# Other blocks with seven products for eight, exponentials three steps later, and norm rows in 8 KB tiles

## The chip, the cores and the metric

The kernel runs on one core of a Trainium2 chip. The metric is the device time of one execution in microseconds, the median of several runs. TensorE multiplies matrices, VectorE and ScalarE do elementwise work, GpSimd does a little of it, and SP (SyncE) issues nearly all transfers from HBM, in the order of the program.

## What is computed

One layer of a streaming encoder over 256 tokens of width 2048, all in float32. With h = layer norm of x, the core of the reference is:

```python
proj = h @ w_in + b_in                       # 2048 x 14400
q, k, v, og, fg, u, z, ga, gb = split(proj)
log_a = log_sigmoid(fg @ w_f2 + b_f2) / 16   # decays, cumulated over chunks of 64 tokens
o = gla_chunk_causal(q, k, v, log_a)         # exp of the decays, states, scores
y_a = rms_norm(o, gla_norm_g) * silu(og)
y_b = gelu(u) * (w_s @ layer_norm(gelu(z), gmlp_ln) + b_s)
m = sigmoid(ga) * y_a + sigmoid(gb) * y_b
h = layer_norm(ALPHA * h + m @ w_o, ln1)
ffn = (silu(gate) * up) @ w_down             # gate, up = split(h @ w_gu), width 5632
ple = sigmoid(h @ w_pg + b_pg) * (p @ w_pu)
out = layer_norm(ALPHA * h + ffn + ple, ln2)
```

## The kernel before

Every weight comes once from HBM in float32, in pieces of 128 x 1024 (two k-tiles of 128 rows by 512 columns). A "split" turns a piece into a high part on ScalarE (a copy to fp32r, L217) and a low part on VectorE (piece minus high part, L218). A product is then three matmuls: high by high, low by high, high by low. A matmul here takes 128 tokens by 512 columns, so a step of `token_block` (one piece, two token halves of 128) has 2 x 2 x 3 = 12 matmuls.

`pair_block` takes two column blocks of 512 at once. For `s` of its k-pairs it forms the 2 x 2 product (token halves by column blocks, over an even and an odd k-tile) with seven products in place of eight, by sums and differences of weights (on VectorE, L448, L480, L483, in place in the raw tile) and of activations (made once per stage by `sums`, on VectorE and one ScalarE copy, L378). The remaining k-pairs go the plain way (`std`). The steps of a seven-product group are short: five splits, a to e, whose steps have 3 to 9 matmuls; two PSUM banks are seeded from a third by ScalarE copies (L414), and two are copied out (L419). This front part of a block is called its head below. The last plain step of a pair block is held back (`pending`) and put behind the first steps of the next block.

The whole program is a list of steps (`steps`), walked by `pump`. Step by step it emits splits ahead, as long as `limit["hl"]` split tiles are in use, and loads ahead, as long as `limit["raw"]` raw tiles are. `before(c, fn)` hangs work before step c, `soon(n, fn)` n steps behind the steps added so far, and `later(n, fn)` n steps behind the one being walked. Evacuations of PSUM are `jobs`, one or two behind each step. SP and GpSimd run in the order in which the program emits; the other engines are ordered by the framework's scheduler from the priorities of that order.

All large tiles (raw and split weights, activations, sums) are slots of one ring of 21 tiles of 8 KB per partition (`slot`, NSLOT). Work tiles of 2 KB come from a ring of nine (`t2`, NT2). A bias or norm row, broadcast to 128 partitions for two column blocks (1024 columns), is a 4 KB tile from a ring of three (`rowvec`, tag "bc", L109 to L115), loaded by SP at L114; a load into this ring waits on SP until the tile's last reader is done, and SP's later loads wait behind it.

The order of the stages is: start (norm of x, transposes), v, fg (two steps, after which the decays are computed piecemeal: `decay_logits`, `decay_log`, `decay_scan`, `decay_ends`, `decay_exp` at set steps), q, k, og with the attention between its steps, z, u, gb, ga, wo, pu, pg, and then four parts of gate/up blocks (gu) followed by the part's down blocks (dn). `residual` scales the normed stream by its gain and adds its bias on GpSimd (L634, L635), four operations per column block, for ln0 during v and q, and for ln1 during pg. Before the change seven products are used with s = 2 in the last two blocks of og, in u, gb, the first two blocks of ga, and the last two of pg, and with s = 3 in gu; v, z, wo and down go the plain way.

Of the kernel before, what the change touches and what calls it, by code (L numbers as in the profile page):

```python
# [42 lines left out]
def block_kernel(ctx: ExitStack, tc: tile.TileContext, x, p, ln0_g, ln0_b, w_in, b_in, w_f2, b_f2,  # L43
# [251 lines left out]
    def token_block(src, nk, xT, evac, name, held=None, halves=False):  # L295

        flush()
        st = {"w": {}}  # L300
# [12 lines left out]

        def size(i):
            return min(KC, nk - i * KC)

        def mk(i):
            def consume(hi, lo):
                if i == 0:
                    st["ps"] = [acc(f"{name}_{t}") for t in range(NT)]  # L320
                st["w"][i] = (hi, lo)
                keep = h0_ <= i < h1_
                final = i == nchunk - 1
                one(i, size(i), 0)
                if final:
                    if keep:
                        evac(0, st["ps"][0])
                    else:
                        jobs.append(lambda: evac(0, st["ps"][0]))
                if not keep:  # L330
                    one(i, size(i), 1)
                elif i == h1_ - 1 and halves:
                    for j in range(2):
                        ps = st["ps"][1] if j == 0 else acc(f"{name}_1b")
                        for ii in range(h0_, h1_):
                            one(ii, size(ii), 1, j * 256, (j + 1) * 256, ps)
                        evac(1, ps, j)
# [199 lines left out]
    def soon(n, fn):  # L537
        before(len(steps) + n, fn)
# [122 lines left out]
    def ws_job():  # L661
# [9 lines left out]
        nc.scalar.activation(wsT[0], wt, AF.Copy)  # L671
        nc.vector.tensor_tensor(out=wsT[1], in0=wt, in1=wsT[0].bitcast(F32), op=ALU.subtract)


    def v_evac(b):
        def evac(t, ps, add=None):
            if "v" not in G:
                G["v"] = [[slot(f"v{i}_{tt}", F32R) for tt in range(NT)] for i in range(2)]
            a = t2(f"av{b}_{t}")
            nc.vector.tensor_tensor(out=a, in0=ps, in1=rowvec("bv", b_in, C_V, b), op=ALU.add)  # L680
            vh, vl = (x[t][:, b * CB:(b + 1) * CB] for x in G["v"])
            nc.scalar.activation(vh, a, AF.Copy)
# [136 lines left out]
    def decay_ends():  # L819
# [5 lines left out]
        for m in range(NCH - 1):  # L825
            nc.vector.tensor_copy(es[:, :, m, m + 1], be[:, :, m + 1])
            for n in range(m + 2, NCH):
                nc.vector.tensor_tensor(out=es[:, :, m, n], in0=es[:, :, m, n - 1], in1=be[:, :, n],
                                        op=ALU.add)
        nc.scalar.activation(es, es, AF.Exp, scale=1.0 / TAU)  # L830
        G["es"], G["be"] = es, be

    def decay_exp(i):
        (mn, lg), be = G["dec"], G["be"]
        n = 4 * NCH
        sl = slice(i * 1024, (i + 1) * 1024)
        bev = be.rearrange("p t n -> p (t n)")[:, i * n:(i + 1) * n].unsqueeze(2).broadcast_to([P, n, CH])
        m = mn[:, sl].rearrange("p (g c) -> p g c", c=CH)
        nc.vector.tensor_tensor(out=m, in0=bev, in1=m, op=ALU.subtract)
        nc.scalar.activation(lg[:, sl], mn[:, sl], AF.Exp, scale=1.0 / TAU)  # L840

    def decay_steps():
        later(2, decay_logits)
# [149 lines left out]
            nc.vector.tensor_tensor(out=y, in0=y, in1=a, op=ALU.mult)  # L993
        return evac

    def s0():
        return G["s0"]
# [5 lines left out]
    before(len(steps) - 3, lambda: G.update(s0=sums(h0T, S_IN, "s0")))  # L1003
    before(len(steps), lambda: limit.update(raw=4, hl=5))
    pairs(w_in, C_OG, h0T, og_evac, "og", S_IN, s0, (2,), [("b_og", b_in, C_OG)])

    def z_evac(b):
        def evac(t, ps, add=None):
            if b == 0 and t == 0:
# [4 lines left out]
            nc.vector.bn_stats(out=st[:, 0, :], in_=a)  # L1014
            mv, r = ln_finish(st, 1, f"zln{b}_{t}")
            nc.vector.scalar_tensor_tensor(out=a, in0=a, scalar=mv[:, 0:1],
                                           in1=rowvec("gmg", gm_g, 0, b), op0=ALU.subtract,
                                           op1=ALU.mult)
            nc.vector.scalar_tensor_tensor(out=a, in0=a, scalar=r[:, 0:1],
                                           in1=rowvec("gmb", gm_b, 0, b), op0=ALU.mult, op1=ALU.add)  # L1020

            w = []

# [14 lines left out]
            later(11, mix)  # L1038
        return evac

    pairs(w_in, C_Z, h0T, z_evac, "z", S_Z, s0, (0, 2), [("b_z", b_in, C_Z), ("gmg", gm_g, 0), ("gmb", gm_b, 0)])

    def yb_evac(key, c0, b, fn):
        def evac(t, ps, add=None):
# [3 lines left out]
            nc.vector.tensor_tensor(out=y, in0=y, in1=a, op=ALU.mult)  # L1048
        return evac

    pairs(w_in, C_U, h0T, lambda b: yb_evac("u", C_U, b, AF.Gelu), "u", S_IN, s0, (0, 2), [("b_u", b_in, C_U)])
    pairs(w_in, C_GB, h0T, lambda b: yb_evac("gb", C_GB, b, AF.Sigmoid), "gb", S_IN, s0, (0, 2), [("b_gb", b_in, C_GB)])

    def ga_evac(b):
# [31 lines left out]
                ln_norm(h0[t], h0[t], st1[t], f"ln1_{t}")  # L1086
        return evac

    for b in range(4):
        token_block(wcols(w_o, b * CB), KT, lambda: G["mT"], wo_evac(b), f"wo{b}",  # L1090
                    held=(4, 8) if b == 3 else None)

# [117 lines left out]
        nc.sync.dma_start(out[t * P:(t + 1) * P, 3 * CB:], y[:, 3 * CB:])  # L1210

    def down_evac(b, last):
        def evac(t, ps, half=None):
            c0, c1 = (0, CB) if half is None else (half * 256, (half + 1) * 256)
            r = r1[t][:, b * CB:(b + 1) * CB]
            nc.vector.tensor_tensor(out=r[:, c0:c1], in0=r[:, c0:c1], in1=ps[:, c0:c1], op=ALU.add)
            if last:
                for c in range(c0, c1, 256):
                    nc.vector.bn_stats(out=st2[t][:, (b * CB + c) // 256, :], in_=r[:, c:c + 256])
# [29 lines left out]
    pump(8)
    with tc.manual_schedule(engines={ET.Activation}):  # L1250
# [33 lines left out]
```

## Time and profile before

| | us |
|---|---|
| median of 3 runs | 1605.48 (1602.62 to 1607.34) |
| the profiled execution, own time | 1605.97 |
| its span in the trace | 1603.8 |
| TensorE busy | 1565.2 (98%) |
| VectorE busy | 1159.4 (72%) |
| ScalarE busy | 817.5 (51%) |
| GpSimd busy | 92.5 (6%) |

Busy times are sums over the span, and the stages differ in which engine is short. TensorE's ends are modelled, so the number of matmuls in a stretch says more than its busy share. The granted clock of TensorE was 0.99 of full over the span. All transfers together moved 315 MB, 197 GB/s in the mean.

### The profile page before, as it was taken

The numbers are of one execution on the slowest core, as the hardware profiler recorded it, in microseconds if no ns is written. First come the engines' busy times: TensorE is split into PE (matmuls) and PEld (weight loads), VectorE is DVE, ScalarE is ACT, GpSimd is POOL, SyncE is SP. The second block draws the span as 40 slices with busy tenths as digits, with TensorE's granted clock in tenths as the row PEclk, the third lists the DMA queues.
The fourth block names the chain that finished last, engine by engine and source line by source line (L and its number), as shares of the span: only waits on it lengthen the run. The fifth ranks groups of instructions, "written<-read, shape, count | busy, mean of one in ns | idle before, by whom it ended". The sixth has DMA issues, their size and how long they took to land.

```text
span 1603.8 us, 19476 instructions
## 1 busy us (share of the span) xinstructions
PE 1565.2 (98%) x7393; PEld 1306.4 (81%) x7393; DVE 1159.4 (72%) x1359; ACT 817.5 (51%) x1026; POOL 92.5 (6%) x69
## 2 busy tenths in 40 slices
PE   8998999999999999999979999999999999999996
PEld 7888988888788888888858788888888888888885
DVE  7668448856888887673897787578775888658875
ACT  5445446644655655542635656445553565535650
POOL 1022000001100000000360000000000000000002
PEclk9999999999999999999989999999999999999998
DMA  8554545765565656674635565545575455755561
GB/s 303 199 190 149 198 153 195 278 230 165 189 205 209 205 194 231 207 246 145 209 119 209 210 210 213 183 156 183 210 262 179 149 187 195 262 184 180 190 233 53
DMA packets 160568, 315.45 MB, mean 197 GB/s; under 512 B 9789, under 2 KB 12762, under 8 KB 160218
## 3 DMA queue, kind: packets, MB, share of 16 engines
q1 hardware_dynamic: 160410, 314.18, 57.1%
q8 instruction: 58, 0.95, 0.2%
q14 instruction: 36, 0.29, 0.1%
q10 hardware_dynamic: 64, 0.02, 0.0%
HBM read 312.06 MB, written 2.10 MB: 196 GB/s over the span
## 4 chain that ended last, share of the span: by engine, by line
issue 48%; PE 22%; POOL 2%; DVE 2%; DMA 1%; ACT 0%; SPq 0%; POOLq 0%
PE gb_C L408 5%; PE u_C L408 5%; PE ga_C L408 3%; PE wo L293 2%; PE wo L291 2%; PE wo L292 2%; PE ga L292 1%; PE ga L291 1%; PE ga L293 1%; POOL xs L635 1%; POOL xs L634 1%; DVE xs L1206 0%; DMA ln1g<-in_ln_g_dram 0%; DVE xs L1204 0%; PE mtp L574 0%
## 5 line engine op out<-in xcount | busy, mean ns | idle before, releaser
L218 DVE TENSOR_TENSOR w_s<-raw,w_s 128x1024 fp32r<-128x1024 f32 x464 | 564.4, 1231 | 283.6 <-ACT w_s L217 280.6
L217 ACT ACTIVATE w_s<-raw 128x1024 fp32r<-128x1024 f32 x464 | 482.8, 1056 | 396.2 <-PE dn L293 94.4
L408 PE MATMUL gu_C<-w_s,h1Th 128*128 128x512 f32 x880 | 283.7, 390 | 0.2
L408 PEld LDWEIGHTS gu_C<-w_s,h1Th 128*128 128x128 f32 x880 | 165.0, 188 | 35.2 <-DVE w_s L218 1.4
L408 PE MATMUL gu_C<-w_s,h1Tl 128*128 128x512 f32 x440 | 171.6, 390 | 0.0
L292 PE MATMUL dn<-w_s,act 128*128 128x512 f32 (+1 forms) x352 | 136.5, 388 | 0.0
L293 PE MATMUL dn<-w_s,act 128*128 128x512 f32 (+1 forms) x352 | 136.2, 387 | 0.0
L291 PE MATMUL dn<-w_s,act 128*128 128x512 f32 (+1 forms) x352 | 136.2, 387 | 0.0
L408 PEld LDWEIGHTS gu_C<-w_s,h1Tl 128*128 128x128 f32 x440 | 82.6, 188 | 17.1
L408 PE MATMUL z_C<-w_s,h0Th 128*128 128x512 f32 x256 | 79.6, 389 | 0.0
L291 PEld LDWEIGHTS dn<-w_s,act 128*128 128x128 f32 x352 | 66.1, 188 | 13.5
L293 PEld LDWEIGHTS dn<-w_s,act 128*128 128x128 f32 x352 | 66.1, 188 | 13.4
L292 PEld LDWEIGHTS dn<-w_s,act 128*128 128x128 f32 x352 | 66.1, 188 | 13.2
L557 POOL TENSOR_TENSOR ln_r<-ln_v,mhalf 128x1 f32<-128x1 f32 x6 | 4.2, 694 | 1115.9 <-DVE ln_v L552 1115.9
L408 PE MATMUL u_C<-w_s,h0Th 128*128 128x512 f32 x192 | 62.4, 396 | 2.4 <-DVE w_s L218 2.4
L408 PE MATMUL gb_C<-w_s,h0Th 128*128 128x512 f32 x192 | 61.1, 389 | 0.0
L448 DVE TENSOR_TENSOR raw<-raw 128x1024 f32<-128x1024 f32 x47 | 58.5, 1266 | 0.5
L408 PEld LDWEIGHTS z_C<-w_s,h0Th 128*128 128x128 f32 x256 | 48.1, 188 | 9.9
L292 PE MATMUL v<-w_s,h0Tl 128*128 128x512 f32 x128 | 50.0, 390 | 0.9 <-POOL h0Tl L581 0.9
L291 PE MATMUL v<-w_s,h0Th 128*128 128x512 f32 x128 | 50.4, 394 | 0.0
L291 PE MATMUL wo<-w_s,mTh 128*128 128x512 f32 x128 | 50.0, 391 | 0.0
L293 PE MATMUL v<-w_s,h0Th 128*128 128x512 f32 x128 | 49.9, 391 | 0.0
(485 smaller groups left out, 3218.1 us busy)
## 6 DMA issues: line engine op xcount, KB each, us to landing
raw<-in_w_in_dram SPq DMA_DIRECT2D x226, 512.0 KB, 4.7
raw<-in_w_gu_dram SPq DMA_DIRECT2D x176, 512.0 KB, 4.5
raw<-in_w_down_dram SPq DMA_DIRECT2D x88, 512.0 KB, 5.0
raw<-in_w_o_dram SPq DMA_DIRECT2D x32, 512.0 KB, 4.8
raw<-in_w_pg_dram SPq DMA_DIRECT2D x32, 512.0 KB, 5.0
xs<-in_x_dram SPq DMA_DIRECT2D x4, 512.0 KB, 5.0
raw<-in_w_pu_dram SPq DMA_DIRECT2D x4, 512.0 KB, 4.4
out_dram<-xs SPq DMA_DIRECT2D x8, 256.0 KB, 2.0
```

Of the source, the lines that this page charges most:

```text
L217: nc.scalar.activation(hi, src, AF.Copy)
L218: nc.vector.tensor_tensor(out=lo, in0=src, in1=hi.bitcast(F32), op=ALU.subtract)
L291: nc.tensor.matmul(ps, lhsT=xh, rhs=wh, start=start, stop=False, **kw)
L292: nc.tensor.matmul(ps, lhsT=xl, rhs=wh, start=False, stop=False, **kw)
L293: nc.tensor.matmul(ps, lhsT=xh, rhs=wl, start=False, stop=stop, **kw)
L408: nc.tensor.matmul(ps, lhsT=a, rhs=b, start=first and j == 0 and n == 0, stop=n == 2, skip_group_check=True)
L448: nc.vector.tensor_tensor(out=r[:, 0:4:2, :], in0=r[:, 0:4:3, :], in1=r[:, 2, :].unsqueeze(1).broadcast_to([P, 2, CB]), op=ALU.subtract)
L557: nc.gpsimd.tensor_tensor(out=r[:, :n], in0=v[:, :n], in1=mhalf[:, :n], op=ALU.pow)
L634: nc.gpsimd.tensor_tensor(out=y, in0=y, in1=gt, op=ALU.mult)
L635: nc.gpsimd.tensor_tensor(out=y, in0=y, in1=bt, op=ALU.add)
```

## The change

- Seven products for eight, `s` of them: v's last two blocks (2), wo's first two (2), and in down one per pair of blocks for all parts but the last two blocks of the last part. Not any more in pg (all four blocks are token blocks) and the first two blocks of u.
- `sums` is called for v, wo and each part of down as well; for gu it stays in pg, before the first step of pg's last block.
- The limits of raw and split tiles are set to 4 and 5 around the new blocks, to 5 and 5 at the head of each part of gu.
- The three exponentials of the decays are issued three steps later.
- The rows of ln0, ln1 and of z's norm are loaded by `row2`: gain and bias for two column blocks lie in one slot of the big ring. The ring of 4 KB rows has two tiles in place of three, the ring of work tiles seven in place of nine, the big ring 22 in place of 21.

```diff
-S_IN, S_Z, S_GA, S_PG, S_FF = 2, 0, 2, 2, 3
+S_V, S_IN, S_U0, S_GA, S_WO, S_PG, S_FF, S_DN = 2, 2, 0, 2, 2, 0, 3, 1
-NSLOT = 21
-NT2 = 9
+NSLOT = 22
+NT2 = 7
@@ rowvec
-            rows_t[k] = tmp.tile([P, 2 * CB], F32, tag="bc", name=f"{key}{b // 2}", bufs=3)
+            rows_t[k] = tmp.tile([P, 2 * CB], F32, tag="bc", name=f"{key}{b // 2}", bufs=2)
+    def row2(name, srcs, i, b):
+        k = name, b // 2
+        if k not in rows_t:
+            rows_t[k] = slot(f"{name}r{b // 2}")
+            for j, src in enumerate(srcs):
+                o = b // 2 * 1024
+                nc.sync.dma_start(rows_t[k][:, j * 1024:(j + 1) * 1024],
+                                  src[o:o + 1024].partition_broadcast(P))
+        return rows_t[k][:, i * 1024 + b % 2 * CB:i * 1024 + (b % 2 + 1) * CB]
@@ residual
-        gt, bt = rowvec(f"{name}g", g, 0, c), rowvec(f"{name}b", b, 0, c)
+        gt, bt = (row2(name, (g, b), i, c) for i in range(2))
@@ v
-    for b in range(4):
+    for b in range(2):
         token_block(wcols(w_in, C_V + b * CB), KT, h0T, v_evac(b), f"v{b}", held=(0, 2) if b == 0 else None)
+        before(len(steps) - 4, lambda: G.update(s0=sums(h0T, S_V, "sv")))
+        before(len(steps), lambda: limit.update(raw=4, hl=5))
+        pairs(w_in, C_V, h0T, v_evac, "v", S_V, s0, (2,), [("bv", b_in, C_V)])
+        flush()
+        before(len(steps), lambda: limit.update(raw=3, hl=4))
@@ decay_ends, decay_exp
-        nc.scalar.activation(es, es, AF.Exp, scale=1.0 / TAU)
+        later(3, lambda: nc.scalar.activation(es, es, AF.Exp, scale=1.0 / TAU))
-        nc.scalar.activation(lg[:, sl], mn[:, sl], AF.Exp, scale=1.0 / TAU)
+        later(3, lambda: nc.scalar.activation(lg[:, sl], mn[:, sl], AF.Exp, scale=1.0 / TAU))
@@ z, u
-    pairs(w_in, C_Z, h0T, z_evac, "z", S_Z, s0, (0, 2), [("b_z", b_in, C_Z), ("gmg", gm_g, 0), ("gmb", gm_b, 0)])
+    soon(8, lambda: gm_row(0, 0))
+    pairs(w_in, C_Z, h0T, z_evac, "z", 0, s0, (0,), [("b_z", b_in, C_Z)])
+    soon(8, lambda: gm_row(0, 2))
+    pairs(w_in, C_Z, h0T, z_evac, "z", 0, s0, (2,), [("b_z", b_in, C_Z)])
-    pairs(w_in, C_U, h0T, ..., "u", S_IN, s0, (0, 2), [("b_u", b_in, C_U)])
+    pairs(w_in, C_U, h0T, ..., "u", S_U0, s0, (0,), [("b_u", b_in, C_U)])
+    pairs(w_in, C_U, h0T, ..., "u", S_IN, s0, (2,), [("b_u", b_in, C_U)])
@@ wo
-    for b in range(4):
+    before(len(steps) - 5, lambda: G.update(sm=sums(G["mT"], S_WO, "sm")))
+    before(len(steps), lambda: limit.update(raw=4, hl=5))
+    pairs(w_o, 0, lambda: G["mT"], wo_evac, "wo", S_WO, lambda: G["sm"], (0,))
+    flush()
+    before(len(steps), lambda: limit.update(raw=3, hl=4))
+    for b in range(2, 4):
@@ pg
-    for b in range(2):
+    for b in range(4):
+        if b == 2:
+            soon(3, lambda: rowvec("b_pg", b_pg, 0, 2))
         token_block(wcols(w_pg, b * CB), KT, h1T_get, pg_evac(b), f"pg{b}", ...)
-    before(len(steps) - 4, lambda: G.update(s1=sums(h1T["x"], S_FF, "s1")))
-    before(len(steps), lambda: limit.update(raw=S_FF + 2, hl=5))
-    pairs(w_pg, 0, h1T_get, pg_evac, "pg", S_PG, s1, (2,), [("b_pg", b_pg, 0)])
+    before(len(steps) - 8, lambda: G.update(s1=sums(h1T["x"], S_FF, "s1")))
@@ each part of gu and down
+        before(len(steps), lambda: limit.update(raw=S_FF + 2, hl=5))
...
+        if S_DN:
+            before(len(steps) - 6, lambda part=part: G.update(sd=sums(G["act", part], S_DN, f"sd{part}")))
+            before(len(steps), lambda: limit.update(raw=4, hl=5))
+        for b in (0, 2):
+            if S_DN and (part < 3 or b == 0):
+                pair_block(src[b:b + 2], npair * 4, act,
+                           (down_evac(b, part == 3), down_evac(b + 1, part == 3)),
+                           f"dn{part}_{b}", S_DN, lambda: G["sd"])
+        if part < 3 and S_DN:
+            continue
-        for b in range(4):
+        for b in range(2 if S_DN else 0, 4):
```

The evacuations of v and down take the copied-out bank as a further addend (`add`), one more VectorE operation in two of four evacuations of a pair.

## Rows read from the trace of the kernel before

**Rows 1.** The page's totals: busy us, share of the span, instructions, by engine.
```profile
PE 1565.2 (98%) x7393; PEld 1306.4 (81%) x7393; DVE 1159.4 (72%) x1359; ACT 817.5 (51%) x1026; POOL 92.5 (6%) x69
```
**Rows 2.** TensorE's waits: line, releaser, us in total, times, longest.
```profile
PE pg_C L408 <- ACT pg_C L414: 4.4, 1, 4.4
PE q L292 <- DVE w_s L218: 4.0, 2, 2.6
PE pg_C L408 <- DVE pg_b_s L218: 2.5, 1, 2.5
PE u_C L408 <- DVE w_s L218: 2.4, 1, 2.4
PE pg L293 <- DVE w_s L218: 2.3, 1, 2.3
...
PE gu_C L408 <- ACT gu_c_s L217: 0.3, 1, 0.3
```
**Rows 3.** Stretches: busy (count) of PE, PEld, DVE, ACT, POOL; PEclk, DMA, GB/s.
```profile
140.00:160.00 20.00, 15.99 (x119) 15.58 (x118) 18.75 (x42) 7.34 (x10) 4.66 (x5) 0.91 0.25 80
410.00:430.00 20.00, 17.10 (x67) 13.38 (x66) 18.51 (x31) 11.74 (x18) 4.29 (x4) 0.91 0.47 155
813.00:843.00 30.00, 19.55 (x64) 14.33 (x63) 28.38 (x25) 12.67 (x16) 14.82 (x8) 0.77 0.45 150
880.00:895.00 15.00, 14.60 (x62) 11.14 (x61) 14.66 (x21) 8.92 (x13) 0.00 (x0) 1.00 0.42 144
502.00:582.00 80.00, 80.00 (x354) 66.26 (x353) 63.70 (x71) 46.73 (x57) 0.00 (x0) 1.00 0.67 230
...
180.00:203.00 23.00, 23.00 (x194) 23.00 (x193) 10.86 (x13) 8.24 (x8) 0.00 (x0) 1.00 0.53 179
```
**Rows 4.** SP's queue in pg, in order of time: start, us, entry.
```profile
786.59 7.73 SPq L226 DMA_DIRECT2D raw<-in_w_pg_dram  x6
808.77 0.34 SPq L114 DMA_DIRECT2D ln1g<-in_ln_g_dram  x1
...
814.57 30.95 SPq L226 DMA_DIRECT2D raw<-in_w_pg_dram  x10
```
**Rows 5.** ScalarE in pg, in order of time, idle time in brackets.
```profile
814.51 1.49 ACT L378 ACTIVATE s_sh<-s_f 128x1536 fp32r<-128x1536 f32 x1 [14.32 <-DVE s_f L372]
```
**Rows 6.** VectorE in pg, in order of time.
```profile
795.99 1.21 DVE L218 TENSOR_TENSOR w_s<-raw,w_s 128x1024 fp32r<-128x1024 f32 x1
...
800.73 3.47 DVE L1149 TENSOR_TENSOR a_pg<-a_pg,pu 128x512 f32<-128x512 f32 x2
...
807.51 2.84 DVE L360 TENSOR_TENSOR s_full<-h1Th,h1Tl 128x1536 f32<-128x1536 f32 x1
...
816.04 2.29 DVE L379 TENSOR_TENSOR s_sl<-s_f,s_sh 128x1536 fp32r<-128x1536 f32 x1 [1.62 <-ACT s_sh L378]
818.25 2.28 DVE L218 TENSOR_TENSOR w_s<-raw,w_s 128x1024 fp32r<-128x1024 f32 x1
```
**Rows 7.** GpSimd in pg: the first and the last of 16 operations.
```profile
787.04 11.31 POOL L634 TENSOR_TENSOR xs<-xs,ln1g 128x512 f32<-128x512 f32 x1 [21.62 <-DMA ln1g<-in_ln_g_dram]
...
827.34 2.13 POOL L635 TENSOR_TENSOR xs<-xs,ln1b 128x512 f32<-128x512 f32 x1
```
**Rows 8.** VectorE's groups, 1000 to 1100 us: busy us, mean ns, idle before.
```profile
L218 DVE TENSOR_TENSOR w_s<-raw,w_s 128x1024 fp32r<-128x1024 f32 x34 | 41.4, 1223 | 28.9 <-ACT w_s L217 28.9
...
L448 DVE TENSOR_TENSOR raw<-raw 128x1024 f32<-128x1024 f32 x3 | 3.6, 1220 | 0.0
...
L480 DVE TENSOR_TENSOR raw<-raw 128x512 f32<-128x512 f32 x3 | 2.0, 682 | 0.0
```
**Rows 9.** VectorE's scans, 132 to 147 us and 147 to 150 us.
```profile
L816 DVE TENSOR_TENSOR_SCAN dmn<-dmn,dlg 128x64 f32<-128x64 f32 x24 | 12.1, 573 | 1.1 <-ACT dlg L810 1.1
...
L816 DVE TENSOR_TENSOR_SCAN dmn<-dmn,dlg 128x64 f32<-128x64 f32 x8 | 1.6, 260 | 0.0
```
**Rows 10.** The last exponential on ScalarE and its reader on VectorE.
```profile
175.75 1.05 ACT L840 ACTIVATE dlg<-dmn 128x1024 f32<-128x1024 f32 x1
...
191.94 1.66 DVE L888 SCALAR_TENSOR_TENSOR kT<-k,rows_cols,dlg 128x256 f32<-128x256 f32 x4 [5.61 <-PE k L293]
```

More of the change, by code (lines that the diff above doesn't have):

```diff
@@ L336, in consume @@
                             one(ii, size(ii), 1, j * 256, (j + 1) * 256, ps)
-                        evac(1, ps, j)
+                        evac(1, ps, half=j)
                 elif i == h1_ - 1:
@@ L672, in ws_job, with s0 @@
         nc.vector.tensor_tensor(out=wsT[1], in0=wt, in1=wsT[0].bitcast(F32), op=ALU.subtract)
+    def s0():
+        return G["s0"]
     def v_evac(b):
@@ L679, in evac @@
             a = t2(f"av{b}_{t}")
+            if add is not None:
+                nc.vector.tensor_tensor(out=a, in0=ps, in1=add, op=ALU.add)
+                ps = a
             nc.vector.tensor_tensor(out=a, in0=ps, in1=rowvec("bv", b_in, C_V, b), op=ALU.add)
@@ L684, in v_evac @@
         return evac
-    for b in range(4):
+    for b in range(2):
         token_block(wcols(w_in, C_V + b * CB), KT, h0T, v_evac(b), f"v{b}", held=(0, 2) if b == 0 else None)
+    if S_V:
+        before(len(steps) - 4, lambda: G.update(s0=sums(h0T, S_V, "sv")))
[3 more added lines that the diff above has]
+        before(len(steps), lambda: limit.update(raw=3, hl=4))
+    else:
+        for b in range(2, 4):
+            token_block(wcols(w_in, C_V + b * CB), KT, h0T, v_evac(b), f"v{b}")
     for c in range(4):
@@ L994, in og_evac @@
         return evac
-    def s0():
-        return G["s0"]
     soon(4, lambda: rowvec("b_og", b_in, C_OG, 0))
@@ L1005, in block_kernel, with gm_row @@
     pairs(w_in, C_OG, h0T, og_evac, "og", S_IN, s0, (2,), [("b_og", b_in, C_OG)])
+    def gm_row(i, b):
+        return row2("gm", (gm_g, gm_b), i, b)
     def z_evac(b):
@@ L1016, in evac @@
             nc.vector.scalar_tensor_tensor(out=a, in0=a, scalar=mv[:, 0:1],
-                                           in1=rowvec("gmg", gm_g, 0, b), op0=ALU.subtract,
+                                           in1=gm_row(0, b), op0=ALU.subtract,
                                            op1=ALU.mult)
             nc.vector.scalar_tensor_tensor(out=a, in0=a, scalar=r[:, 0:1],
-                                           in1=rowvec("gmb", gm_b, 0, b), op0=ALU.mult, op1=ALU.add)
+                                           in1=gm_row(1, b), op0=ALU.mult, op1=ALU.add)
             w = []
@@ L1049, in yb_evac @@
         return evac
-    pairs(w_in, C_U, h0T, lambda b: yb_evac("u", C_U, b, AF.Gelu), "u", S_IN, s0, (0, 2), [("b_u", b_in, C_U)])
+    pairs(w_in, C_U, h0T, lambda b: yb_evac("u", C_U, b, AF.Gelu), "u", S_U0, s0, (0,), [("b_u", b_in, C_U)])
+    pairs(w_in, C_U, h0T, lambda b: yb_evac("u", C_U, b, AF.Gelu), "u", S_IN, s0, (2,),
+          [("b_u", b_in, C_U)])
     pairs(w_in, C_GB, h0T, lambda b: yb_evac("gb", C_GB, b, AF.Sigmoid), "gb", S_IN, s0, (0, 2), [("b_gb", b_in, C_GB)])
@@ L1087, in wo_evac @@
         return evac
-    for b in range(4):
+    before(len(steps) - 5, lambda: G.update(sm=sums(G["mT"], S_WO, "sm")))
[3 more added lines that the diff above has]
+    before(len(steps), lambda: limit.update(raw=3, hl=4))
+    for b in range(2, 4):
         token_block(wcols(w_o, b * CB), KT, lambda: G["mT"], wo_evac(b), f"wo{b}",
@@ L1212, in down_evac, with evac @@
     def down_evac(b, last):
-        def evac(t, ps, half=None):
+        def evac(t, ps, add=None, half=None):
             c0, c1 = (0, CB) if half is None else (half * 256, (half + 1) * 256)
@@ L1216, in evac @@
             nc.vector.tensor_tensor(out=r[:, c0:c1], in0=r[:, c0:c1], in1=ps[:, c0:c1], op=ALU.add)
+            if add is not None:
+                nc.vector.tensor_tensor(out=r, in0=r, in1=add, op=ALU.add)
             if last:
@@ L1240, in block_kernel @@
         before(len(steps) + (npair - 1) * 2, lambda: run_jobs(100))
-        for b in range(4):
-            src = w_down[k_first * P:(k_first + npair * 4) * P, b * CB:(b + 1) * CB].rearrange(
-                "(kt p) c -> p kt c", p=P)
+        src = [w_down[k_first * P:(k_first + npair * 4) * P, b * CB:(b + 1) * CB].rearrange(
+            "(kt p) c -> p kt c", p=P) for b in range(4)]
+        act = lambda part=part: G["act", part]
+        if S_DN:
[9 more added lines that the diff above has]
+        for b in range(2 if S_DN else 0, 4):
             last = part == 3 and b == 3
@@ L1246, in block_kernel @@
                 before(len(steps) - 6, load_gb2)
-            token_block(src, npair * 4, lambda part=part: G["act", part], down_evac(b, part == 3),
+            token_block(src[b], npair * 4, act, down_evac(b, part == 3),
                         f"dn{part}_{b}", held=(0, 4) if last else None, halves=last)
```

## The prediction

> **What bounds the kernel now.** I read the page's totals first: TensorE is busy 98% of the span [rows 1], so only two things can shorten it, fewer matmuls or less time in which TensorE stands still or runs slowly. The second view is TensorE's own list of waits [rows 2]. It is short, and the reader is to see that nearly all of it lies at three places: q (4.0 us), the first u block (2.4), and pg (4.4, 2.5 and 2.3). The third view, busy time by stretch, prices these places in full, half clock included, because it counts matmuls [rows 3]. In the undisturbed gb stretch 354 matmuls of 512 columns take 80 us, 0.226 us each; in the late q and k stretch 194, all of 256 columns, take 23 us, 0.119 us each. What a stretch takes beyond its count is lost:
>
> - q, 140 to 160 us: 20.0 - 119 x 0.119 = 5.8 us.
> - z to u, 410 to 430: 20.0 - 67 x 0.226 = 4.9 us.
> - pg, 813 to 843: 30.0 - 64 x 0.226 = 15.5 us, at a granted clock of 0.77 on average (part of it at 1.2 GHz in place of 2.4).
> - gu0, 880 to 895: 15.0 - 62 x 0.226 = 1.0 us.
>
> Together 27 us, against some 1,560 us of matmuls. The fourth view is what the other engines did there. In pg, SP issued six weight loads by 794.3 us, and its next entry, a row tile of ln1, left at 808.8, after a wait of 14.4 us for one of three row buffers; the weight loads behind it left from 814.6 on [rows 4]. ScalarE stood for 14.3 us before its copy in `sums` (L378) [rows 5], because VectorE's six operations of `sums` ran from 807.5 to 818.3, each beside the residual on GpSimd [rows 6, 7]. So three things meet in pg: `sums`, the residual's rows in SP's queue, and the head of a seven-product block, which wants many splits for few matmuls.
>
> **The change part by part.**
>
> *Matmuls.* A seven-product group (one pair of k-tiles, two token halves, two column blocks) has 7 x 3 = 21 matmuls in place of 24, so it saves 3. Added groups: v 2, wo 2, down seven blocks of 1: 11, so -33 matmuls. Removed: pg 2, u0 2: +12. Net -21 x 0.226 = **-4.7 us**. No other matmul changes, and all these lie on the path, TensorE being the bound.
>
> *pg.* It becomes four plain blocks; `sums` moves from 12 to 24 steps behind pg's start, 12 x 12 x 0.226 = 32.5 us later: from 807.5 to about 840, when the residual, which ended at 829.5, is over. It issues no DMA; the ln1 rows come, two loads at a time as before, in two 8 KB slots of the big ring, which at that place has room (xs 2, pu 2, h1T 4, raw 3, split 4 and rows 2 make 17 of 22). SP's 14.4 us wait and ScalarE's 14.3 us wait go. What is late next is VectorE beside GpSimd: the 16 residual operations remain (787.0 to 829.5 us) [rows 7]. Beside them a split takes 2.28 us where one just before took 1.21, and a 512-column product 1.73 where 0.68 is the free price [rows 6, 8]. A plain block asks in 8 x 12 x 0.226 = 21.7 us for 8 x 2.28 + 4 x 1.73 + 2 x 0.69 = 26.5 us of VectorE. Over the 31 us of overlap VectorE falls 7 us behind; its lead is three steps, 8.1 us. Bounds: nothing is lost, or 7 us and a stretch at 1.2 GHz like the one between 410 and 430, (1 - 0.91) x 20 = 1.8 us. I take 2.5, near the lower end because the lead covers the sum: **-13.0 us**.
>
> Here a rule of the Trainium skill speaks against the change. The rows show that VectorE's operation with two SBUF inputs and GpSimd's residual each wait for the other: 1.21 became 2.28 us, and one GpSimd operation stood 11.3 us while VectorE ran without a gap [rows 6, 7]. The page "SBUF — State Buffer", section "Who interferes with whom", says that these two share a port as an exclusive lock, held for a whole instruction, which agrees. By it, moving `sums` and the rows frees no port, and pg would keep its contention; that is the first rival below.
>
> *u0.* Plain, it spares VectorE two groups' extra: 2 x (1.22 + 0.68 + 0.68) for the combinations and 2 x 1.5 x 1.22 for the extra splits = 8.8 us [rows 8]. The 4.9 us lost there is u's splits lying behind z's last evacuations on VectorE [rows 2]. What is late next is the head of u2, 16 x 12 x 0.226 = 43 us later, when z's work is long done. Bounds 0 to 4.9 of gain; I take 3.9: **-3.9 us**.
>
> *Decays and ln0 rows.* The last ln0 residuals now run at steps 40 and 45, while the scans start at 48 (v has six steps more); before, they ran at the same two steps with the scans at 42 to 49, and 24 scans, half of them beside GpSimd, took 12.1 us where the last eight, alone, took 1.6 [rows 9]. Alone, 24 take 4.8, so some 7 us of VectorE go; but the rows' slot comes late if the big ring is full there (23 wanted of 22, by my count of live tiles; 22 of 21 before), and the residual slides into the scans again. Bounds 0 to 5.8 of gain; I take the middle: **-3.0 us**. The exponentials go three steps later: 3 x 24 x 0.119 = 8.6 us. The last ended at 176.8, its reader on VectorE began at 191.9 [rows 10]: 6.5 us are left, so this costs and gains nothing. Were that margin gone, two PSUM banks would wait, of five.
>
> *New heads.* v, wo and seven blocks of down get a head of short steps, and v, wo and four parts of down a `sums`. Per group VectorE gets 2.6 us of combinations and 1.8 of splits; `sums` with one group is a third of the six operations that took 10.8 us under contention [rows 6, 8], and none of the new ones lies beside the residual. No row shows a one-group block or a seven-product block of down. Nearest rows: eleven gu heads, with waits of 0.3 us in all and a loss of 1.0 at the first [rows 2, 3]; the other end is a head like u0's, 4.9. I take 0.25 each, as most gu heads had VectorE at like load: 9 x 0.25 = **+2.3 us**.
>
> *Buffers.* Two row buffers for three, seven work tiles for nine, 22 slots for 21: the row waits of ln0, gm and ln1 leave SP's short ring for the big one, behind which the weight loads stand as before. Bounds: a wait like the 14.4 us one comes back and costs TensorE up to pg's 15.5 us, or the same amount is spared elsewhere, where I have counted it. I take 0; the upper end is a rival.
>
> **Sum.** -4.7 - 13.0 - 3.9 - 3.0 + 2.3 = -22.3 us. The profiled execution took 1605.97 us (span 1603.8), 0.5 above the median of 1605.48. So 1605.5 - 22.3 = 1583.2, forecast **1583 us**.
>
> **Rivals.**
>
> 1. *Contention keeps pg late* (VectorE and GpSimd in each other's way). For: the 16 GpSimd operations stay beside plain splits. Against: the lead of 8.1 us is larger than the lag of 7. Price: 7 + 1.8 in place of 2.5, so +6.3: 1590.
> 2. *The stalls in q and at u only move*, to the scans after a late slot and to u2's head. For: VectorE's total work grows. Against: u0's plain steps give 43 us of air. Price 3.9 + 3.0: 1590.
> 3. *Row tiles starve the weight ring.* A row tile in the big ring waits for a slot, and SP's weight loads wait behind it. For: 23 of 22 at the decays, 22 at z. Against: slots turn over at every step of 2.7 us, a row buffer only after its last reader. Price one more stall of pg's size, 15.5: 1599.
> 4. *Slower: the heads of down.* A head asks ScalarE and VectorE for five splits and two seeds before TensorE may go on; where VectorE is behind, each costs what u0's head cost, 4.9 us. Nine of them: 1583.2 + 9 x (4.9 - 0.25) = 1625. It decides from 22.3 / 9 + 0.25 = 2.7 us per head on. For: pg's own head, of the three stalls in rows 2 the worst. Against: eleven larger heads of gu pass [rows 2].
>
> **Numbers.** The likeliest case has 0.50, rival 1 0.13, rival 2 0.10, rival 3 0.12, rival 4 0.13; 0.02 is for anything else. The low end is all 27.2 us gone and 4.7 us of matmuls, with heads free: 1605.5 - 31.9 = 1573.6, so 1573; the high end takes in rival 3: 1602. Within 0.3% (4.8 us), about what a measurement of this kernel can tell from no change, counts as the same: rival 3 lies at that edge, half of it (0.06) and the rest (0.02) go there. Faster: 0.50 + 0.13 + 0.10 + 0.06 = 0.79; same 0.08; slower 0.13.
>
> **What would show it.** Right: TensorE's count falls by 21 to 7372; the waits of pg_C and of u_C are gone from its list; SP's longest wait for GpSimd at a row tile falls from 14.4 us to a few; the granted clock in pg stays at 1.0 (2.4 GHz); the q wait is under 2 us. Wrong, by step: a wait of pg for a split during the residual (rival 1); q's wait still at 4 (rival 2); SP's weight loads waiting long behind a row tile at z, ln0 or ln1 (rival 3); TensorE waiting for ScalarE's seeds or VectorE's splits at dn_C, wo_C or v_C (rival 4), with the clock falling to 1.2 GHz behind them. A time above 1602 makes the prediction wrong in its sign.

## The result and the profile after

The changed kernel takes 1590.97 us (median of four runs, 1588.32 to 1593.27) against 1605.69 for the kernel before on the same chip (1602.62 to 1607.34): ratio 0.991, 95% interval 0.9888 to 0.9932. That is 14.7 us faster, where the prediction's sum had 22.3. The profiled execution has a span of 1588.9 us, 14.9 below the 1603.8 of before.

The page's totals after, which answer to [rows 1]: busy us, share of the span, instructions.

```profile
PE 1555.8 (98%) x7372; PEld 1300.6 (82%) x7372; DVE 1212.1 (76%) x1451; ACT 848.7 (53%) x1081; POOL 89.3 (6%) x69
```

There are 7372 matmuls, the 21 fewer that were counted. VectorE has 53 us more to do and 15 us less to do it in.

TensorE's waits after, which answer to [rows 2] (line, releaser, us in total, times, longest):

```profile
PE v_C L419 <- ACT v_C L425: 2.6, 1, 2.6
PE v_C L419 <- DVE w_s L229: 2.6, 2, 1.4
...
PE f_ps L819 <- DVE dmn L826: 2.0, 1, 2.0
PE v_C L419 <- DVE v_b_s L229: 1.6, 1, 1.6
...
PE v_C L419 <- ACT v_b_s L228: 1.2, 1, 1.2
PE gu_C L419 <- ACT gu_C L425: 1.1, 1, 1.1
PE pg L303 <- DVE h1Tl L592: 1.0, 1, 1.0
```

The waits of pg_C, u_C and q are gone. Four kinds of wait at v_C stand in their place, in a stage that before had only a wait of 0.9 us at its start (v, for h0Tl); f_ps, in the decays, is new too. Before the matmuls of wo_C and dn_C the trace shows no idle time of TensorE.

The stretches after, which answer to [rows 3] (length; busy us and count on PE, PEld, DVE, ACT, POOL; granted clock, DMA share, GB/s): v's head, v's last products, fg and the decays, q, z to u, pg, gu0.

```profile
58.00:80.00 22.00, 16.55 (x57) 12.29 (x56) 16.13 (x19) 10.24 (x14) 0.00 (x0) 0.77 0.22 75
100.00:115.00 15.00, 12.41 (x54) 9.62 (x53) 11.02 (x7) 5.53 (x7) 11.80 (x7) 1.00 0.62 206
115.00:140.00 25.00, 22.26 (x139) 19.98 (x138) 21.64 (x24) 10.54 (x17) 16.07 (x11) 0.93 0.40 141
140.00:160.00 20.00, 20.00 (x169) 20.00 (x169) 17.73 (x49) 13.68 (x17) 0.00 (x0) 1.00 0.56 193
410.00:430.00 20.00, 20.00 (x90) 16.53 (x90) 17.11 (x30) 10.16 (x13) 4.87 (x4) 1.00 0.57 184
813.00:843.00 30.00, 30.00 (x134) 24.86 (x133) 29.43 (x23) 13.10 (x15) 14.59 (x8) 1.00 0.67 222
865.00:885.00 20.00, 18.89 (x84) 15.30 (x83) 19.86 (x26) 13.53 (x18) 0.00 (x0) 1.00 0.43 154
```

Priced as in the prediction, at 0.226 us for each 512-column matmul. The pg stretch, which lost 15.5 us with 64 matmuls, holds 134 and loses nothing; z to u holds 90 and loses nothing; q holds 169 small ones in 20 us and loses nothing. But v's head lost 22.0 - 57 x 0.226 = 9.1 us and v's last products 15.0 - 54 x 0.226 = 2.8, in two stretches where TensorE was never idle before:

```profile
58.00:80.00 22.00, 22.00 (x99) 18.22 (x98) 12.89 (x13) 9.20 (x10) 0.00 (x0) 1.00 0.70 245
100.00:115.00 15.00, 15.00 (x98) 13.72 (x97) 10.45 (x9) 4.93 (x7) 11.96 (x8) 1.00 0.59 200
```

From 115 to 140 us, where matmuls of both widths are mixed, TensorE stands 2.7 us and has the clock at 0.93, up to 0.07 x 25 = 1.8 us more, so about 4.5 are lost there by this estimate. A stretch that loses nothing is called whole below.

v's head, in order of time, first VectorE, then ScalarE (start, us, line, operation; in brackets the idle time ahead and its releaser):

```profile
58.48 0.69 DVE L229 TENSOR_TENSOR v_a_s<-raw,v_a_s 128x512 fp32r<-128x512 f32 x1 [2.04 <-DMA raw<-in_w_in_dram]
62.75 0.69 DVE L697 TENSOR_TENSOR av<-v,bv 128x512 f32<-128x512 f32 x1 [3.58 <-PE v L304]
63.36 1.21 DVE L459 TENSOR_TENSOR raw<-raw 128x1024 f32<-128x1024 f32 x1
64.49 0.68 DVE L697 TENSOR_TENSOR av<-v,bv 128x512 f32<-128x512 f32 x1
65.09 1.21 DVE L459 TENSOR_TENSOR raw<-raw 128x1024 f32<-128x1024 f32 x1
```

```profile
64.60 1.06 ACT L228 ACTIVATE v_b_s<-raw 128x1024 fp32r<-128x1024 f32 x1 [6.16 <-DVE raw L459]
```

And SP's queue in the same place:

```profile
39.79 13.25 SPq L237 DMA_DIRECT2D raw<-in_w_in_dram  x4
53.14 1.80 SPq L670 DMA_DIRECT2D wf<-in_w_f_dram  x4
55.03 26.60 SPq L237 DMA_DIRECT2D raw<-in_w_in_dram  x6
```

SP's wait in it:

```profile
SPq L237 <- PE v L304: 10.1, 1, 10.1
```

The chain reads from the bottom up. SP's weight loads come apart: the four entries from 39.79 on take 13.25 us because SP stands 10.1 us for a slot that TensorE has not yet left. The second pair's weights land late, and VectorE stands 2.04 us for them. Its next entry is the evacuation of the plain block v1 (L697), which can't start until TensorE has finished that block: 3.58 us idle. Only behind it comes the head's weight difference (L459), and ScalarE stood 6.16 us for that before the split which TensorE needs.

### The profile page after: what moved, and what is told of

The parts are those of the page before. It is cut to its first block, busy times and chain, and to the rows that moved or that the text cites. A ratio compares the mean times of both kernels' runs of the same rounds, so it can differ in the third digit from the quotient of the medians.

```text
span 1588.9 us, 19560 instructions
## 1 busy us (share of the span) xinstructions
PE 1555.8 (98%) x7372; PEld 1300.6 (82%) x7372; DVE 1212.1 (76%) x1451; ACT 848.7 (53%) x1081; POOL 89.3 (6%) x69
## 4 chain that ended last, share of the span: by engine, by line
issue 48%; PE 44%; DVE 5%; DMA 1%; POOL 1%; ACT 1%; SPq 0%; DVEq 0%; ACTq 0%; POOLq 0%
PE z_C L419 5%; PE u_C L419 5%; PE gb_C L419 5%; PE ga_C L419 3%; PE og_C L419 3%; PE wo_C L419 3%; PE v_C L419 2%; DVE w_s L229 2%; PE k L304 1%; PE k L303 1%; PE k L302 1%; PE og L303 1%; PE og L304 1%; PE q L303 1%; PE q L304 1%
## 5 line engine op out<-in xcount | busy, mean ns | idle before, releaser
L228 ACT ACTIVATE w_s<-raw 128x1024 fp32r<-128x1024 f32 x450 | 466.1, 1055 | 301.8 <-DVE w_s L229 69.2
L419 PE MATMUL dn_C<-w_s,act 128*128 128x512 f32 x792 | 186.1, 390 | 0.0
L419 PEld LDWEIGHTS dn_C<-w_s,act 128*128 128x128 f32 x792 | 148.4, 188 | 30.6
L459 DVE TENSOR_TENSOR raw<-raw 128x1024 f32<-128x1024 f32 x54 | 65.1, 1220 | 0.6
L303 PE MATMUL pg<-w_s,h1Tl 128*128 128x512 f32 x128 | 50.0, 390 | 1.0 <-DVE h1Tl L592 1.0
L302 PE MATMUL pg<-w_s,h1Th 128*128 128x512 f32 x128 | 50.1, 391 | 0.0
L304 PE MATMUL pg<-w_s,h1Th 128*128 128x512 f32 x128 | 49.9, 390 | 0.0
L419 PE MATMUL z_C<-w_s,h0Tl 128*128 128x512 f32 x128 | 49.8, 389 | 0.0
L419 PEld LDWEIGHTS u_C<-w_s,h0Th 128*128 128x128 f32 x224 | 42.0, 188 | 8.8
L228 ACT ACTIVATE gu_b_s<-raw 128x1024 fp32r<-128x1024 f32 x33 | 34.1, 1055 | 23.1 <-PE gu_C L419 7.9
L419 PE MATMUL u_C<-w_s,h0Tl 128*128 128x512 f32 x112 | 43.6, 389 | 0.0
L419 PEld LDWEIGHTS gb_C<-w_s,h0Th 128*128 128x128 f32 x192 | 36.0, 188 | 7.5
```

The costliest lines, as they stand in the source:

```text
L228: nc.scalar.activation(hi, src, AF.Copy)
L302: nc.tensor.matmul(ps, lhsT=xh, rhs=wh, start=start, stop=False, **kw)
L303: nc.tensor.matmul(ps, lhsT=xl, rhs=wh, start=False, stop=False, **kw)
L304: nc.tensor.matmul(ps, lhsT=xh, rhs=wl, start=False, stop=stop, **kw)
L419: nc.tensor.matmul(ps, lhsT=a, rhs=b, start=first and j == 0 and n == 0, stop=n == 2, skip_group_check=True)
L459: nc.vector.tensor_tensor(out=r[:, 0:4:2, :], in0=r[:, 0:4:3, :], in1=r[:, 2, :].unsqueeze(1).broadcast_to([P, 2, CB]), op=ALU.subtract)
```

## Experiments

All twelve kernels ran in three rounds beside the kernel before, whose median was 1605.5 to 1605.7 us each time; each ratio is to it. Unless stated, an edit is made to the changed kernel.

**Is the whole loss of 9.1 + 2.8 us v's seven products?** e1 makes v plain.

```diff
-S_V, S_IN, ... = 2, 2, 0, 2, 2, 0, 3, 1
+S_V, S_IN, ... = 0, 2, 0, 2, 2, 0, 3, 1
```

> The changed kernel with v's last two blocks plain again (no sums there, 6 matmuls more, +1.4 us). Theory A (the loss in v comes from the new head: its sums and the plain work around it fill the ring of 8 KB tiles) and theory B (any seven-product head in v overloads VectorE) both say that the 9.1 us lost at 58 to 80 us go: 1591 - 9.1 + 1.4 = 1583. The 2.8 us at 100 to 115 may stay, since the residual on GpSimd then still runs beside v's evacuations. Rival C (v was always going to lose this there, to wf and the rows): 1591 or more.

Measured 1580.35 us (1580.32 to 1581.66), ratio 0.9843 [0.9829, 0.9858]: 10.6 better than the change as a whole, though it has six matmuls more. v's seven products gain 1.4 us of matmuls and lose 12 as a balance over the kernel: with v plain the stretch of fg is whole too, but q loses 20.0 - 135 x 0.119 = 3.9 us. What is left lost is q, to which a wait comes back, and the first head of gu:

```profile
PE q L303 <- DVE w_s L229: 3.5, 2, 2.6
PE gu_C L419 <- ACT gu_C L425: 2.3, 1, 2.3
```

**Why is v's head late?** Either the ring is full there (the slots of `sums` and of wf, the tile with w_f2, keep the weight loads waiting), or a head of short steps is simply too much for VectorE behind plain steps. e2 frees both kinds of slot, e9 and e10 one each.

```diff
-before(len(steps) - 4, lambda: G.update(s0=sums(h0T, S_V, "sv")))   # e2, e9
+before(len(steps) - 8, lambda: G.update(s0=sums(h0T, S_V, "sv")))
-before(14, wf_job)                                                  # e2, e10
+before(34, wf_job)
```

> The changed kernel with v's sums issued at step 8 in place of 12 and the wf tile at step 34 in place of 14, so that four 8 KB slots are not taken just when the weights of v's seven-product head should load. Theory A (full ring) says that the 9.1 us at 58 to 80 fall to 3 or less: 1584. Theory B (VectorE cannot prepare a head fast enough there, whatever the ring) says 1591, with the stall where it was.

> Leaves nothing out; the kernel after with the sums of v four steps sooner, wf's loads where they were. If the sums' three slots are what fills the ring at v's head: the SP wait of 10.1 us for a slot goes, v's head loses 2 us in place of 9, time 1583.6 as with both parts together. If wf's slot is it: head unchanged, 1591. If each takes one slot of two that are wanted: about 1587.

> Leaves nothing out; the kernel after with wf loaded at step 34 in place of 14, the sums where they were. If wf's slot is what is lacking at v's head: head loss 2 us in place of 9, time 1583.6. If the sums' slots are: head unchanged, 1591. If each takes one of two slots that are wanted: about 1587.

Measured: e2 1583.63 us (1580.16 to 1586.01), ratio 0.986 [0.9843, 0.9877]; e9 1586.63 (1584.47 to 1588.55), 0.9883 [0.9866, 0.9899]; e10 1587.92 (1587.26 to 1591.17), 0.9892 [0.9878, 0.9907]. The stretch of v's head in e2, e9 and e10:

```profile
58.00:80.00 22.00, 21.06 (x91) 16.55 (x90) 19.19 (x22) 14.18 (x20) 0.00 (x0) 1.00 0.44 150
```

```profile
58.00:80.00 22.00, 21.07 (x90) 16.54 (x90) 19.29 (x22) 14.33 (x20) 0.00 (x0) 1.00 0.52 166
```

```profile
58.00:80.00 22.00, 16.49 (x56) 12.19 (x55) 16.54 (x19) 10.14 (x13) 0.00 (x0) 0.77 0.29 96
```

With the sums four steps sooner 90 or 91 matmuls fit where 57 did, and the loss is 1.4 to 1.7 us in place of 9.1; with wf late alone nothing moves there. So the sums' place is the cause of the head's loss, and wf is not. The seven-product work is the same, so a head as such isn't too much for VectorE. In e9 SP's longest wait on plain v falls from 10.1 to 5.3 us, and VectorE has the two L459 ahead of the evacuation (L697) and no idle time there for TensorE:

```profile
59.59 1.23 DVE L459 TENSOR_TENSOR raw<-raw 128x1024 f32<-128x1024 f32 x1
...
62.60 0.68 DVE L697 TENSOR_TENSOR av<-v,bv 128x512 f32<-128x512 f32 x1
```

The slot and the order of VectorE's queue changed together; which of them alone would do was not separated.

By the totals alone e9 and e10 meet the third expectation, 1587 for each; the trace tells otherwise. e9 gains 7 us at the head and loses part of them behind it, as e2 does (TensorE busy 18.76 and 18.27 of the 20 us from 80 on, 20.00 in the changed kernel). e10 gains nothing at the head and 3 us elsewhere. The stretch of fg and the decays, which in e9 (first row) loses as much as in the changed kernel, is whole again in e10 but for 0.1 us (second row); against that gain of 4.4 stand 1.4 lost again at v's last products (third row, 15.0 - 48 x 0.226 = 4.2 us lost):

```profile
115.00:140.00 25.00, 22.48 (x157) 20.88 (x157) 19.54 (x23) 16.02 (x23) 13.17 (x9) 0.93 0.40 138
115.00:140.00 25.00, 24.89 (x170) 22.65 (x169) 22.37 (x24) 12.20 (x19) 16.61 (x11) 1.00 0.48 169
100.00:115.00 15.00, 12.60 (x48) 9.44 (x48) 10.67 (x7) 4.87 (x7) 11.87 (x8) 0.89 0.61 215
```

The wait of f_ps (2.0 us) is gone from e10's list, and still in e9's. So two stalls lie in this part, and each has its own cure: a total that fits a theory was not enough to tell them apart. Whether wf's slot or its loads in SP's queue matter at fg was not separated.

**What costs 2.8 us behind the head and 4.5 at fg?** The ln0 residual on GpSimd runs there. e3 moves it into k, e5 into z (with v plain), e11 into z with e2's edits.

```diff
-before(30 + 5 * c, lambda c=c: residual(ln0_g, ln0_b, c, "ln0"))
+before(58 + 3 * c, ...)                  # e3
+before((105, 108, 112, 115)[c], ...)     # e5, with S_V = 0
+before((111, 114, 118, 121)[c], ...)     # e11, with e2's edits
```

> The changed kernel with ln0's residual on GpSimd at steps 58 to 67 (in k, where VectorE is half idle) in place of 30 to 45. If VectorE beside GpSimd is what loses the 2.8 us at 100 to 115 and the 4 to 5 us at 116 to 140 (fg, decays), these fall to 1 or 2 and the time to 1585. If the order of the decays or the ring loses them, they stay: 1591. If the residual then hurts k in the same way: 1588 to 1592 with new waits of k.

> The changed kernel with v plain and ln0's residual moved from steps 30 to 45 (v3, fg, q) into the first z blocks (steps 105 to 115), which are plain and where VectorE is busy 25 of 40 us. With v plain alone 4.8 us are still lost in q (110 to 160 us), where the decays run beside the residual. If that is the cause: 1580.4 - 4.8 + 1.3 (what pg's plain blocks still lose beside ln1's residual) = 1577. If the loss only moves again, as it did into the attention when the residual ran in k: 1580 to 1584, with new waits of z or og. If q's loss is the decays themselves: 1580 or more, waits of q as they were.

> Leaves nothing out; v's sums early, wf late, and the ln0 residual moved to the z blocks. If the 6 us that are still lost between 90 and 110 us come from the residual on GpSimd beside v's evacuations and the residual costs z nothing: 1583.6 - 6.1 = 1577.5. If the residual costs z what it cost with v plain (TensorE lost 6.1 us there): 1583.6, the loss is moved.

Measured: e3 1591.60 us (1589.68 to 1594.19), ratio 0.9913 [0.9898, 0.9927]; e5 1580.69 (1580.39 to 1584.8), 0.9849 [0.9834, 0.9864], no better than e1; e11 1581.43 (1581.34 to 1581.94), 0.9849 [0.9834, 0.9863]. Two stretches of e3, fg and the decays, and k with the first scores:

```profile
115.00:140.00 25.00, 25.00 (x189) 23.61 (x188) 14.71 (x20) 15.82 (x22) 0.00 (x0) 1.00 0.34 110
215.00:235.00 20.00, 15.25 (x74) 12.94 (x73) 12.80 (x25) 9.39 (x21) 0.05 (x1) 0.83 0.51 173
```

The loss leaves the place that the residual leaves (from 100 to 115 us e3 is whole too), and appears in the place to which it goes. At fg the residual alone is not enough, though: in e10 it is still there (GpSimd busy for 16.61 us) and the stretch is whole. e11's time lies between its two expectations. In it q and fg are whole and z loses 20.0 - 64 x 0.226 = 5.5 us:

```profile
350.00:370.00 20.00, 15.99 (x64) 12.76 (x63) 11.83 (x20) 7.57 (x10) 9.60 (x7) 0.91 0.58 205
```

Who waits tells how. In e11's z these are SP's queue, ScalarE, VectorE and TensorE in turn (first four rows); in e3's k it is ScalarE (the last):

```profile
SPq L237 <- POOL xs L646: 12.9, 1, 12.9
```

```profile
ACT w_s L228 <- DMA raw<-in_w_in_dram: 9.5, 1, 9.5
DVE w_s L229 <- ACT w_s L228: 9.1, 3, 7.5
...
PE z_C L419 <- DVE a_z L1011: 4.0, 1, 4.0
```

```profile
ACT w_s L228 <- POOL xs L646: 7.7, 1, 7.7
```

`POOL xs L646` is the residual's last read of a row tile. In the changed kernel a row tile is one of the big ring's slots, and a weight load or a split whose turn it is for that slot waits until GpSimd is done. In e11 GpSimd's last read ends at 357.8 us; the load that stood for it lands and ScalarE's split starts at 361.7, VectorE's at 362.7, z's evacuation behind that at 363.9, and TensorE, which waited 4.0 us for it, goes on at 364.6. This is the prediction's third rival with its order turned round: here not the row tile waits for a slot, but the weights wait for the slot that it holds. It is found at k and at z; at fg of the changed kernel ScalarE waits 3.6 us in the same way, but how much of the loss there is due to that was not separated.

At v's last products the price is another one, VectorE's own time. From 100 to 160 us its splits take 1.57 us on average in the changed kernel (first row), and 1.22 in e3 (second row), where the residual does not run beside them; TensorE's two waits for w_s there (2.6 us together) are for such splits, and they are gone from e3's list. Here too it takes two: before the change, beside plain blocks of v, the residual (11.96 us of GpSimd from 100 to 115 us, in the row shown with the result) cost TensorE nothing.

```profile
L229 DVE TENSOR_TENSOR w_s<-raw,w_s 128x1024 fp32r<-128x1024 f32 x19 | 29.4, 1570 | 1.7 <-ACT w_s L228 1.6
```

```profile
L229 DVE TENSOR_TENSOR w_s<-raw,w_s 128x1024 fp32r<-128x1024 f32 x23 | 27.3, 1220 | 5.4 <-ACT w_s L228 5.4
```

With row tiles of their own the same residual lost 5.8 us at q too [rows 3], which also says that the slots are not the only price; small row tiles for ln0 alone were not tried.

**Which part of pg's three made its loss?** e4 makes pg plain in the kernel before, with the `sums` for gu at its end, and keeps the small row tiles. e8 gives the changed kernel the seven-product pg again, with its `sums` where they were.

```diff
-for b in range(2):                                                  # e4; e8 the reverse
+for b in range(4):
     token_block(wcols(w_pg, b * CB), KT, h1T_get, pg_evac(b), f"pg{b}", ...)
-before(len(steps) - 4, lambda: G.update(s1=sums(h1T["x"], S_FF, "s1")))
...
-pairs(w_pg, 0, h1T_get, pg_evac, "pg", S_PG, s1, (2,), [("b_pg", b_pg, 0)])
+before(len(steps) - 8, lambda: G.update(s1=sums(h1T["x"], S_FF, "s1")))
...
```

> The kernel before with pg's four blocks plain and gu's sums at pg's last block, nothing else changed: the rows of ln1 still in three 4 KB tiles. If sums and the head of the seven-product block lose the 15.5 us in pg, nearly all comes back, against 6 matmuls more: 1605.5 - 14.2 + 1.4 = 1593. If SP's wait for a row tile (14.4 us) loses it, half or more stays: 1599 or above, with the weight loads still late at 808 us.

> The changed kernel with pg's last two blocks at seven products and sums at step 12 of pg, as before the change (6 matmuls fewer), while ln1's rows stay in slots of the big ring, so that SP does not wait for a row tile. If sums and the head beside the residual lose the 15.5 us: 1591 - 1.4 + 14.2 = 1604, weight loads in time. If SP's wait of 14.4 us had a part in it: 1590 + 7 or less, 1597 or below.

Measured: e4 1591.32 us (1589.65 to 1592.62), ratio 0.9907 [0.9891, 0.9924]; e8 1606.75 (ten runs, 1604.18 to 1607.95), 1.0003 [0.9993, 1.0012]. SP's longest wait in e4's pg, then pg's stretch in e4 and in e8:

```profile
SPq L114 <- POOL xs L634: 22.5, 2, 14.4
```

```profile
785.00:850.00 65.00, 65.00 (x288) 53.81 (x288) 55.58 (x46) 27.73 (x30) 37.11 (x16) 1.00 0.63 217
```

```profile
785.00:850.00 65.00, 53.58 (x216) 42.12 (x215) 63.16 (x61) 28.99 (x38) 30.59 (x16) 0.90 0.47 155
```

e4 keeps SP's 14.4 us wait of [rows 4] to the tenth and loses nothing in pg. e8 has the big slots, a longest wait of SP for a row tile of 7.6 us, and loses 65.0 - 216 x 0.226 = 16.2 us. So neither the wait for a row buffer nor the kind of row tile made the loss; the seven-product block with its `sums` beside the residual did, and ScalarE's wait for them is back (14.6 us in e8, 14.3 in [rows 5]). Both edits move the head and its `sums` together; which of the two made the loss was not separated. e4 also shows what all other edits are worth together: 1591.32 without them, 1590.97 with them, no difference that these runs can tell.

**Do u0's and down's parts stand as priced?** e6 gives u0 its seven products back (`S_U0` 2), e7 makes down plain (`S_DN` 0).

> The changed kernel with seven products again in u's first two blocks (6 matmuls fewer, -1.4 us). If its head behind z's last evacuations lost the 4.9 us before, they come back: 1591 - 1.4 + 4.9 = 1594.5, with waits of u_C for splits. If the row tiles of z's norm in the short ring were the cause, which stay in slots here: 1589.6 and no wait.

> The changed kernel with down plain again: 21 matmuls more (+4.7 us), no heads and no sums in down. If the seven new heads of down cost nothing: 1595.7. If they cost the 0.25 us each that was forecast: 1594. If they cost as much as they save: 1591.

Measured: e6 1592.95 us (1592.07 to 1595.23), ratio 0.9922 [0.9907, 0.9936]; e7 1595.02 (1593.45 to 1596.66), 0.9933 [0.9918, 0.9947]. In e6 z to u loses 30.0 - 117 x 0.226 = 3.6 us again, against 1.4 us of matmuls that are saved: 2.2 net, 2.0 measured (the intervals of the two times overlap; the stretch shows the loss).

```profile
400.00:430.00 30.00, 27.08 (x117) 21.70 (x116) 26.34 (x42) 16.18 (x23) 4.34 (x4) 0.99 0.32 104
```

In e7 there are 21 matmuls more, 4.7 us, and the time is 4.1 longer: seven heads of down and their four `sums` cost 0.6 us in all, less than the runs scatter.

**Can the two findings be put together?** e12 leaves v plain and issues gu's `sums` four steps sooner in pg.

```diff
-before(len(steps) - 8, lambda: G.update(s1=sums(h1T["x"], S_FF, "s1")))
+before(len(steps) - 12, lambda: G.update(s1=sums(h1T["x"], S_FF, "s1")))
```

> Leaves nothing out; v plain, and gu's sums four steps sooner in pg. If gu0's head (2.5 us lost with v plain) is late for the sums in VectorE's queue: 1580.4 - 2 = 1578.4, and TensorE's wait for gu's seed falls under 1 us. If it is the splits of the head themselves: 1580.4. If the sums meet the ln1 residual on GpSimd, pg loses some 4 us: 1584.

Measured 1578.64 us (1577.84 to 1580.28), ratio 0.9832 [0.9817, 0.9847]: the fastest of all, 12.3 us under the changed kernel. Against e1 it is 1.7 us lower, with intervals that overlap, but the trace shows the part that moved. The wait of gu_C is gone from its list, and gu0 is whole:

```profile
865.00:885.00 20.00, 20.00 (x90) 16.57 (x89) 18.36 (x22) 14.92 (x20) 0.00 (x0) 1.00 0.76 253
```

## Why the prediction came out as it did

The sign and the large term were right, the sum was 7.6 us too good. That 1590.97 is the 1590 at which rivals 1 and 2 stood is chance: neither of them took the loss to be in v. Term by term, forecast against measured:

| term | forecast | measured | from |
|---|---|---|---|
| matmuls | -4.7 | -4.7 | 7372 instead of 7393 |
| pg | -13.0 | -14.5 | loss 15.5, then the wait of 1.0 for h1Tl |
| u0 | -3.9 | -4.9 | loss 4.9, then 0; in e6 3.6 of it is there again |
| decays, ln0 rows | -3.0 | -1.3 | loss 5.8 at q, then 4.5 at 115 to 140 us |
| new heads | +2.3 | +12.9 | v's head 9.1, v's end 2.8, ahead of wo 0.4, down 0.6 |
| sum | -22.3 | -12.5 | spans -14.9, medians -14.7 |

The last line leaves 2.4 us, of which 0.4 lie ahead of v (its first matmul starts at 15.7 us in place of 16.1); the rest I can't assign. wo's 0.4 is the wait of the transposes ahead of wo for ga's last evacuation (mtp L585, for DVE L1093), not of wo's head; no experiment took wo apart.

**The step that failed is "New heads".** It said that none of the new `sums` "lies beside the residual" and took "0.25 each, as most gu heads had VectorE at like load". For down that was right (0.6 for seven, with their sums). For v it was not, by a factor of 36: the head of v cost 9.1 us. The upper end that I had, 4.9 from u0's head, did not hold it either. gu's heads follow one another; v's stands behind plain blocks, with its `sums` only four steps ahead of it and in the way of the weight loads. Plain blocks ahead are not enough by themselves: wo's head stands behind two as well, with its `sums` five steps ahead, and its matmuls waited for nothing. At v a stall of 3.6 us on VectorE was made longer by order (evacuation, difference, split) and by the clock.

**The rivals.** The fourth, slower by heads, had the right kind of loss at one place out of nine, so the time stayed far from its 1625. The third, row tiles that starve the ring, was given 0.12 at 1599. It is real, in the turned order told above, but at z and k, where experiments put the residual, it cost 5.5 us and 4.8 us of idle time with some of the clock, not 15.5. The first, that contention keeps pg late, did not come. There the rule of the Trainium skill was weighed ("SBUF — State Buffer", section "Who interferes with whom"), by which moving `sums` frees no port. The contention is there, since GpSimd's operations in pg (first row) take 2.0 us on average where one of ln0 (second row) took 1.3, and VectorE is busy 29.43 of 30 us; yet TensorE waits for nothing. That the lead of three steps keeps it from TensorE, as the prediction argued, fits this; no run varied the lead. At v's last products the same contention did reach TensorE.

```profile
L646 POOL TENSOR_TENSOR xs<-xs,ln1r 128x512 f32<-128x512 f32 x8 | 16.0, 2006 | 1.3 <-DMA ln1r<-in_ln_b_dram 0.8
```

```profile
102.29 1.30 POOL L645 TENSOR_TENSOR xs<-xs,ln0r 128x512 f32<-128x512 f32 x1 [52.90 <-DMA ln0r<-in_ln_g_dram]
```

**pg.** The time was near, but one of the three causes that I named was none. I counted SP's wait for a row buffer among what makes the loss; e4 keeps it and loses nothing. In the changed kernel the wait has not gone either, it has another releaser (VectorE's splits, 11.6 us in two, 7.7 the longest). Why it is harmless beside plain blocks was not taken apart. The change of time came from the seven products and `sums` alone, the two together.

**Decays.** The scans came free just as worked out: 32 of them took 6.1 us, 264 ns each, where before 24 took 12.1 and the last eight 1.6 [rows 9].

```profile
L842 DVE TENSOR_TENSOR_SCAN dmn<-dmn,dlg 128x64 f32<-128x64 f32 x32 | 6.1, 264 | 1.0 <-ACT dlg L836 1.0
```

The error was to take the loss of q as what the scans cost. With the scans free q loses nothing, but the residual's second half now runs at fg, from 124 to 137 us, and a loss is there. It takes two to make it: e3, without the residual there, loses nothing from 115 to 140, and e10, with the residual but with wf later, 0.1 us. The second rival, that the stall only moves, was right for this term and wrong for u0.

## What to carry to other kernels

A block that wants preparation (sums, differences of weights) is priced by where its preparation stands in the in-order queues, not by its amount: look at what is queued ahead of it, and whether that waits for the very engine that it feeds. Price a new block by what stands ahead of it at its place, not by later blocks of its kind. When a loss follows a piece of work to each place to which it is moved, ask which buffer it holds, who is next for that buffer, and whom it slows. And check a cure by the stretch that it was meant for: a total can meet the forecast by a gain elsewhere.

## What the runs showed of the hardware

TensorE's granted clock fell during short idle times and stayed down while TensorE was busy again. Four rows of v's head in the changed kernel, 2 us each:

```profile
64.00:66.00 2.00, 0.81 (x4) 0.39 (x3) 2.00 (x3) 1.40 (x2) 0.00 (x0) 1.00 0.00 0
68.00:70.00 2.00, 1.91 (x4) 1.12 (x4) 2.00 (x4) 1.00 (x2) 0.00 (x0) 0.50 0.00 0
70.00:72.00 2.00, 0.17 (x1) 0.00 (x0) 2.00 (x3) 0.39 (x1) 0.00 (x0) 0.50 0.00 0
74.00:76.00 2.00, 2.00 (x6) 1.52 (x6) 1.82 (x2) 0.91 (x2) 0.00 (x0) 0.50 0.24 40
```

From 64 to 66 us TensorE was idle for more than half the time at 2.4 GHz; at 68 the clock stood at 1.2 GHz, and from 74 to 76 TensorE was busy throughout and did six matmuls of 512 columns where it does nine at full clock. In that stretch TensorE's listed waits sum to 5.4 us (2.6, 1.6 and 1.2), and 9.1 were lost: the rest is the clock's.
